# Both feed-forward layers as one level of Strassen, with streamed weights

## The chip, the cores and the metric

The kernel runs on one core of a Trainium2 chip. The metric is the device time of one execution in microseconds; the time shown for a kernel is the median of several executions. Engines are called as in the profile: PE (TensorE; PEld are its weight loads), DVE (VectorE), ACT (ScalarE), POOL (GpSimd) and SP (the queue from which nearly all DMAs are issued).

## What is computed

One step of a decoder layer: a prompt of 2048 tokens and eight single sample tokens go through an input projection, windowed attention, an mLSTM, an output projection and a feed-forward part, with norms between. The change touches the feed-forward part alone. Cut to that, with D_MODEL = 1024 and D_FF = 4096:

```python
x = x + jnp.concatenate([out_a, out_b], axis=-1) @ w_out
h2 = rmsnorm(x, norm2_g)
x = x + jnp.square(jax.nn.relu(h2 @ w_ff1)) @ w_ff2
...
y_prompt = rmsnorm(xp, final_g)
```

All of it is float32. The kernel splits each operand of a matmul into a high part (fp32r, made by ACT) and a low part (the remainder, made by DVE) and adds three matmuls: high by high, high by low and low by high.

## The kernel before

The order of each engine's instructions comes from a scheduler that starts from the order of the program text and from the buffers of the tile pools; each engine then runs its list in that order and waits on semaphores. `bufs=2` means that a name has two buffers in turn: the third tile of that name waits until the first one's readers are done.

The feed-forward part is `phase_c` (L1329). It first runs the output projection of the 16 token tiles of 128 (and one of 8), tile by tile, with the second norm and the transposes of tiles 0 to 7 woven in (`prep_norm`, `prep_move`). The transposed activations h2 stay in SBUF as high and low parts, for one half of the tokens at a time: tiles 0 to 7 as two blocks of 512 tokens, tiles 8 to 16 as blocks of 512, 256 and 264. Tiles 8 to 16 are prepared near the end of the first half's feed-forward work, in small jobs taken from a list (`bg`, `step`).

For each half there are 16 groups g of 256 hidden features. `ff1` (L1410) loads two tiles of w_ff1 (1024x128, 512 KB each, `load_ff`), splits them, and for each token block adds 8 x 3 matmuls in PSUM, applies relu on ACT (L1420), squares on DVE (L1421) and splits the result. `ff2` (L1429) loads two rows of w_ff2, and for each block and each of 8 output tiles adds 2 x 3 matmuls in PSUM; ACT copies the first group's sum to `acc` (L1440), and DVE adds the others' (L1442). ff1 of group g+1 stands ahead of ff2 of group g. A helper records all matmuls (L162 to L164) and splits (L158 on ACT, L159 on DVE).

After a half's last group, `finish` transposes `acc` back, adds the residual (L1457), takes the last norm on DVE (L1463) or on ACT and POOL (L1466), and stores the tile. The first half's tiles are finished inside the second half's work, the last tiles behind the last matmuls. POOL has nothing else to do in this part; in the parts before it, it does element-wise work on tiles of 128 to 640 columns.

## Time and profile before

| | us |
|---|---|
| median of 3 runs | 2720.64 |
| lowest and highest | 2719.99, 2722.58 |
| the profiled execution | 2713.16 |
| its span, first to last instruction | 2711.3 |
| PE busy | 2643.3 |
| DVE busy | 1459.7 |
| ACT busy | 840.4 |
| POOL busy | 200.2 |

The page gives busy times over the whole span, slices of a fortieth of the span each, and the chain that ended last. The view by stretches gives for each stretch its length, the busy time and number of instructions of each engine, the granted PE clock (1.00 is full), the share of time in which DMA engines moved data, and GB/s. In the views by group a row ends with the busy time, the mean duration in ns, and the idle time ahead of the group with what ended it. In the timeline a row begins with start and duration in us; "x2" means two instructions in a row taken together.

### The profile page before, as it was taken

The page shows a single profiled execution, that of the slowest core. Times are in us where ns is not written, and L with a number is a line of the kernel's source. Part 1 is how long each engine was busy: PE and PEld are TensorE (multiplying, and loading weights), DVE is VectorE, ACT ScalarE, POOL GpSimd, SP SyncE. Part 2 cuts the span into 40 slices and gives each one's busy share as a digit, 9 for nine tenths or more (in the row PEclk, how much of TensorE's full clock was granted, in tenths as well). Part 3 has the DMA queues.
Part 4 walks back from the last instruction along what each step waited for, and adds up shares of the span by engine and source line. Part 5 has one row for each costly group of instructions (what it writes and reads, how often), then busy time and mean ns, then how long its engine had stood idle before and what let it go on. Part 6 is the DMA issues. An engine that isn't in the chain of part 4 may idle for free.

```text
span 2711.3 us, 39662 instructions
## 1 busy us (share of the span) xinstructions
PE 2643.3 (97%) x15262; PEld 2333.0 (86%) x15262; DVE 1459.7 (54%) x3434; ACT 840.4 (31%) x1888; POOL 200.2 (7%) x198
## 2 busy tenths in 40 slices
PE   8999999999999989999999999999999999999997
PEld 7999999999788767887888888888889999999996
DVE  6324655665377566753345444444754545454547
ACT  5331224443345443322321212122452121212123
POOL 1000000000253242210000000000000000000001
PEclk9999999999799889999999999999999999999999
DMA  8575576656576565543222222111341111111113
GB/s 199 151 204 157 172 182 140 153 141 156 131 199 162 149 186 170 166 150 111 90 81 64 100 69 63 45 49 47 102 140 55 40 55 40 55 40 55 40 35 123
DMA packets 334225, 302.55 MB, mean 112 GB/s; under 512 B 108543, under 2 KB 301467, under 8 KB 331092
## 3 DMA queue, kind: packets, MB, share of 16 engines
q1 hardware_dynamic: 332212, 296.39, 38.5%
q0 software_dynamic: 1536, 3.10, 0.5%
q8 instruction: 120, 1.97, 0.3%
q14 instruction: 69, 0.57, 0.1%
q10 hardware_dynamic: 288, 0.53, 0.1%
HBM read 220.94 MB, written 95.17 MB: 117 GB/s over the span
## 4 chain that ended last, share of the span: by engine, by line
PE 89%; DVE 5%; DMA 3%; ACT 2%; issue 1%; POOL 0%; SPq 0%; DVEq 0%; ACTq 0%; POOLq 0%
PE pf L163 19%; PE pf L162 19%; PE pf L164 19%; PE pmm L162 5%; PE pmm L164 5%; PE pmm L163 5%; PE ps_s L1074 5%; PE po L1102 3%; PE pt L1087 2%; PE ptp L176 1%; PE ppq L367 1%; PE ppq L370 1%; DMA xt<-x_d 1%; DMA out_dram<-kt 0%; PE nu L459 0%
## 5 line engine op out<-in xcount | busy, mean ns | idle before, releaser
L1442 DVE TENSOR_TENSOR acc<-acc,pf 128x512 f32<-128x512 f32 (+2 forms) x600 | 343.4, 581 | 201.2 <-PE pf L164 200.0
L164 PE MATMUL pf<-rh,w2l 128*128 128x512 f32 (+2 forms) x1280 | 445.3, 348 | 0.0
L163 PE MATMUL pf<-rlo,w2h 128*128 128x512 f32 (+2 forms) x1280 | 445.0, 348 | 0.1
L162 PE MATMUL pf<-rh,w2h 128*128 128x512 f32 (+2 forms) x1280 | 444.4, 348 | 0.0
L162 PEld LDWEIGHTS pf<-rh,w2h 128*128 128x128 f32 x1280 | 241.8, 189 | 30.2 <-ACT rh L158 0.2
L163 PEld LDWEIGHTS pf<-rlo,w2h 128*128 128x128 f32 x1280 | 241.4, 189 | 30.6 <-DVE rlo L159 0.3
L164 PEld LDWEIGHTS pf<-rh,w2l 128*128 128x128 f32 x1280 | 241.3, 189 | 30.1 <-DVE w2l L159 0.2
L162 PE MATMUL pmm<-x,wh 128*128 128x344 f32 (+1 forms) x768 | 251.0, 327 | 0.0
L163 PE MATMUL pmm<-x,wh 128*128 128x344 f32 (+1 forms) x768 | 249.0, 324 | 0.0
L164 PE MATMUL pmm<-x,wl 128*128 128x344 f32 (+1 forms) x768 | 248.3, 323 | 0.0
L162 PE MATMUL pf<-h21h,w1h 128*128 128x512 f32 (+2 forms) x768 | 245.8, 320 | 0.0
L164 PE MATMUL pf<-h21h,w1l 128*128 128x512 f32 (+2 forms) x768 | 245.6, 320 | 0.0
L163 PE MATMUL pf<-h21l,w1h 128*128 128x512 f32 (+2 forms) x768 | 245.2, 319 | 0.0
L158 ACT ACTIVATE rh<-rl 128x264 fp32r<-128x264 f32 (+1 forms) x160 | 87.3, 546 | 465.8 <-PE pf L164 241.7
L163 PE MATMUL pf<-h20l,w1h 128*128 128x512 f32 x512 | 200.0, 391 | 0.0
L162 PE MATMUL pf<-h20h,w1h 128*128 128x512 f32 x512 | 200.0, 391 | 0.0
L164 PE MATMUL pf<-h20h,w1l 128*128 128x512 f32 x512 | 199.4, 390 | 0.0
L159 DVE TENSOR_TENSOR w1l<-w1r,w1h 128x1024 fp32r<-128x1024 f32 x64 | 78.4, 1226 | 186.0 <-ACT w1h L158 186.0
L1076 DVE CUSTOM_DVE_ANT_0 sm<-ps_s,nb 128x256 f32<-128x256 f32 (+1 forms) x288 | 100.0, 362 | 138.2 <-PE ps_s L1074 110.2
L1078 ACT ACTIVATE ex<-sm,R 128x256 f32<-128x256 f32 (+1 forms) x288 | 126.1, 459 | 144.1 <-DVE R L1076 140.3
L1421 DVE TENSOR_TENSOR rl<-rl 128x264 f32<-128x264 f32 (+1 forms) x160 | 93.3, 583 | 141.3 <-ACT rl L1420 141.3
L163 PEld LDWEIGHTS pf<-h21l,w1h 128*128 128x128 f32 x768 | 144.6, 188 | 12.8
(461 smaller groups left out, 5058.6 us busy)
## 6 DMA issues: line engine op xcount, KB each, us to landing
w1r<-in_w_ff_dram SPq DMA_DIRECT2D x64, 512.0 KB
w2r<-in_w_ff_dram SPq DMA_DIRECT2D x64, 512.0 KB
xt<-in_x_prompt_dram SPq DMA_DIRECT2D x31, 512.0 KB
xt<-x_d SPq DMA_DIRECT2D x25, 512.0 KB
R_d<-R SPq DMA_DIRECT2D x72, 132.0 KB
Rb<-R_d SPq DMA_DIRECT2D x48, 198.0 KB
V<-v_d SPq DMA_DIRECT2D x72, 130.0 KB
wraw<-in_w_in_dram SPq DMA_DIRECT2D x17, 512.0 KB
```

Source lines behind the costliest of these rows:

```text
L158: last_hi[0] = act.activation(hi, src, AF.Copy)
L159: last_lo[0] = (eng or vec).tensor_tensor(lo, src, hi.bitcast(F32), op=OP.subtract)
L162: pe.matmul(out, lh, rh, start=first, stop=False)
L163: pe.matmul(out, lh, rl, start=False, stop=False)
L164: pe.matmul(out, ll, rh, start=False, stop=last)
L1074: pe.matmul(out, Q[:, a:a + (P - 1) * d + 1:d], mv, start=i == 0, stop=i == 1)
L1076: vec.tensor_tensor_reduce(sm[:, :w], s_[:, e, c0:c0 + w], nb[:, o + bw - w:o + bw], 1.0, 3e38, OP.add, OP.min, mn)
L1078: act.activation(ex[:, e, :w], sm[:, :w], AF.Exp, bias=mn, scale=-1.0)
L1087: pe.transpose(pt[:, e, kb], ex[:, e, kb * P:(kb + 1) * P], ident)
L1102: pe.matmul(po[:, i + e], pT[:, e, kb], vts[kb], start=kb == 0, stop=kb == nk - 1)
L1421: vec.tensor_tensor(r[:, :n], r[:, :n], r[:, :n], op=OP.mult)
L1442: vec.tensor_tensor(av, av, pf[:, :n], op=OP.add)
```

## The change

Both layers become, for each half of the tokens (now 1024 and 1032), one level of Strassen's scheme. A matrix product of 2x2 blocks is made from 7 products of sums and differences of blocks, in place of 8. The features are worked off in two chunks of 2048, so that a chunk's first layer is a product of 2048 x 1024 (weights) by 1024 x tokens, and its second of 1024 x 2048 by 2048 x tokens, each cut in halves on all sides. What follows from that:

- Weights are streamed: each "step" of 24 matmuls (48 in the second half, whose blocks of 516 tokens are cut in two of 258) loads one or two blocks of 128x1024 (`a_load`, names `ax` and `ay`, two buffers each), adds or subtracts them on POOL where the product asks for two (`combine`; 5 of 7 products), and splits the sum into `ah` and `al`, three buffers each. A product has four steps.
- Activations: h2 of all tiles is made in the output projection and stored to DRAM (`h2_d`). In the first layer each product loads two pieces of 256 rows x half the tokens of one or two blocks (`b_load`, `bx` two buffers, `by` one), adds them on POOL where there are two, and splits them (`b_prep`, `bh` and `bl`, four buffers each). In the second layer the pieces are sums of the hidden blocks `R`, four per product, without loads.
- `ahead(s)` stands before step s: it prepares weights up to step s+2, loads up to s+3, and prepares up to two activation pieces when the piece four before it is used up.
- Results: each product's sum in PSUM is added to or subtracted from one or two blocks of the result (12 in all for 7 products), the first time by a copy on ACT, later on DVE (`put`). Blocks of the first layer get relu and square when complete, two of the four on ACT, two in one instruction on DVE (L1515 of the new kernel, both inputs in SBUF).
- The orders of the products are 5, 1, 2, 3, 6, 4, 7 in the first layer and 5, 3, 1, 2, 6, 4, 7 in the second.

```diff
-    CBLK = (((0, 512), (512, 512)), ((1024, 512), (1536, 256), (1792, 264)))
+    PROD_A = {1: ((0, 0), (1, 1), 1), 2: ((1, 0), (1, 1), 1), 3: ((0, 0), None, 0), 4: ((1, 1), None, 0),
+              5: ((0, 0), (0, 1), 1), 6: ((1, 0), (0, 0), -1), 7: ((0, 1), (1, 1), -1)}
+    PROD_B = {1: ((0, 0), (1, 1), 1), 2: ((0, 0), None, 0), 3: ((0, 1), (1, 1), -1), 4: ((1, 0), (0, 0), -1),
+              5: ((1, 1), None, 0), 6: ((0, 0), (0, 1), 1), 7: ((1, 0), (1, 1), 1)}
...
+    ORDER = {1: (5, 1, 2, 3, 6, 4, 7), 2: (5, 3, 1, 2, 6, 4, 7)}
+    SB = ((0, 512, 1), (1024, 516, 2))
...
+        def a_load(s):
...
+            for (r, q), name in zip([x for x in blocks[:2] if x], ("ax", "ay")):
+                x = wst.tile([P, 4 * 256], F32, name=name, bufs=2)
...
+        def combine(tl, sign):
+            if len(tl) > 1:
+                gp.tensor_tensor(tl[0], tl[0], tl[1], op=OP.add if sign > 0 else OP.subtract)
+            return tl[0]
...
+        def a_split(s):
+            d = steps[s]
+            x = combine(d.pop("raw"), PROD_A[d["p"]][2])
+            h = wst.tile([P, 4 * 256], F32R, name="ah", bufs=3)
+            l = wst.tile([P, 4 * 256], F32R, name="al", bufs=3)
+            split(h, l, x)
...
+        def b_prep(j):
...
+            if u_["ph"] == 1:
+                x = combine(u_.pop("raw"), blocks[2])
+            else:
+                tl = [R[b, u_["j"]][:, :, :W] for b in blocks[:2] if b]
+                x = tl[0]
+                if len(tl) > 1:
+                    x = wst.tile([P, 2, 516], F32, name="bx", bufs=2)[:, :, :W]
+                    gp.tensor_tensor(x, tl[0], tl[1], op=OP.add if blocks[2] > 0 else OP.subtract)
+            h = wst.tile([P, 2, 516], F32R, name="bh", bufs=4)
+            l = wst.tile([P, 2, 516], F32R, name="bl", bufs=4)
+            split(h[:, :, :W], l[:, :, :W], x)
...
+        def ahead(s):
+            while nxt["raw"] < min(s + 4, len(steps)) and nxt["raw"] < nxt["split"] + 2:
+                a_load(nxt["raw"])
+                nxt["raw"] += 1
+            while nxt["split"] < min(s + 3, nxt["raw"]):
+                a_split(nxt["split"])
...
+            for _ in range(2 if s else 4):
+                j = nxt["bprep"]
+                if j == len(bunits) or bunits[j]["first"] > s + 4 or (j >= 4 and bunits[j - 4]["last"] >= s):
+                    break
...
+        def put(dst, src, sign, new, nb):
...
+            if new:
+                act.activation(dst, src, AF.Copy, scale=float(sign))
+            else:
+                vec.tensor_tensor(dst, dst, src, op=OP.add if sign > 0 else OP.subtract)
...
+                        if (blk, p) in (((0, 1), 3), ((1, 0), 4)):
+                            act.activation(cv, cv, AF.Relu)
+                            act.activation(cv, cv, AF.Square)
+                        elif (blk, p) in (((1, 1), 6), ((0, 0), 7)):
+                            vec.scalar_tensor_tensor(cv, cv, 0.0, cv, op0=OP.max, op1=OP.mult)
```

The order shows what this makes of two engines. On POOL, before, the last element-wise work of the output projection (`Rb`) is followed directly by the last norm of the final tiles (`xt`), with the whole feed-forward part between them:

```order
L346 TENSOR_TENSOR Rb_13218<-Rb_13218,dw 128x6x65
L346 TENSOR_TENSOR Rb_13220<-Rb_13220,dw 128x6x65
L346 TENSOR_TENSOR Rb_13325<-Rb_13325,dw 128x6x65
L346 TENSOR_TENSOR Rb_13327<-Rb_13327,dw 128x6x65
L346 TENSOR_TENSOR Rb_13432<-Rb_13432,dw 128x6x65
L346 TENSOR_TENSOR Rb_13434<-Rb_13434,dw 128x6x65
L1466 TENSOR_TENSOR xt_24987<-xt_24987,fg 128x1024
L1466 TENSOR_TENSOR xt_24989<-xt_24989,fg 128x1024
```

On POOL, after, in the second layer of the first half's first chunk, weight sums (`ax`) alternate with activation sums made from the hidden blocks (`bx` from two `R`; the numbers tell the tiles apart):

```order
L1444 TENSOR_TENSOR bx<-R_14068,R_14244 128x2x512
L1444 TENSOR_TENSOR bx<-R_14109,R_14284 128x2x512
L1409 TENSOR_TENSOR ax<-ax,ay 128x1024 x2
L1444 TENSOR_TENSOR bx<-R_13988,R_14164 128x2x512
L1444 TENSOR_TENSOR bx<-R_14029,R_14204 128x2x512
L1444 TENSOR_TENSOR bx<-R_14070,R_14244 128x2x512
L1444 TENSOR_TENSOR bx<-R_14111,R_14284 128x2x512
L1444 TENSOR_TENSOR bx<-R_13988,R_13986 128x2x512
L1409 TENSOR_TENSOR ax<-ax,ay 128x1024 x3
```

There are 280 such sums over the feed-forward part, where there were none.

On DVE, before, in the second half, low parts of weights (`w1l`, `w2l`) and of hidden blocks (`rlo`), squarings (`rl`) and result additions (`acc`) follow each other like this:

```order
L159 TENSOR_TENSOR w2l<-w2r,w2h 128x1024
L1421 TENSOR_TENSOR rl<-rl 128x512
L159 TENSOR_TENSOR rlo_19702<-rl,rh_19701 128x512
L1421 TENSOR_TENSOR rl<-rl 128x256
L159 TENSOR_TENSOR rlo_19734<-rl,rh_19733 128x256
L159 TENSOR_TENSOR w1l<-w1r,w1h 128x1024
L1421 TENSOR_TENSOR rl<-rl 128x264
L159 TENSOR_TENSOR rlo_19766<-rl,rh_19765 128x264
L1421 TENSOR_TENSOR rl<-rl 128x512
L1421 TENSOR_TENSOR rl<-rl 128x256
L159 TENSOR_TENSOR w1l<-w1r,w1h 128x1024
L1442 TENSOR_TENSOR acc<-acc,pf_19883 128x512
```

On DVE, after, in the second layer of the first half, low parts of weight sums (`al`) and of activation sums (`bl`) stand in runs between the result additions:

```order
L160 TENSOR_TENSOR bl<-bx,bh 128x2x512
L160 TENSOR_TENSOR al<-ax,ah 128x1024
L1479 TENSOR_TENSOR acc<-acc,pf_15853 128x512
L1479 TENSOR_TENSOR acc<-acc,pf_15860 128x512
L1479 TENSOR_TENSOR acc<-acc,pf_15867 128x512
L1479 TENSOR_TENSOR acc<-acc,pf_15874 128x512
L160 TENSOR_TENSOR al<-ax,ah 128x1024
L160 TENSOR_TENSOR bl<-bx,bh 128x2x512 x4
L160 TENSOR_TENSOR al<-ax,ah 128x1024
L1479 TENSOR_TENSOR acc<-acc,pf_16007 128x512
```

Each `al` or `bl` with a sum ahead of it waits for that sum on POOL and for the high part on ACT, and the additions behind it on DVE wait with it.

More of the change, by code (lines that the diff above doesn't have):

```diff
@@ new lines, in ahead @@
+        def ahead(s):
[4 more added lines that the diff above has]
+                a_split(nxt["split"])
+                nxt["split"] += 1
+                if nxt["raw"] < min(s + 4, len(steps)):
+                    a_load(nxt["raw"])
+                    nxt["raw"] += 1
+            for _ in range(2 if s else 4):
+                j = nxt["bprep"]
+                if j == len(bunits) or bunits[j]["first"] > s + 4 or (j >= 4 and bunits[j - 4]["last"] >= s):
+                    break
+                if nxt["bload"] == j:
+                    b_load(j)
+                    nxt["bload"] += 1
+                b_prep(j)
+                nxt["bprep"] += 1
+                if j + 1 < len(bunits) and bunits[j + 1]["first"] <= s + 6:
+                    b_load(j + 1)
+                    nxt["bload"] += 1
@@ new lines, in half, with final @@
+        def half(xt, acc, base, t, i):
+            t0, n = t * P, P if t < NT else NB
+            pt = pst.tile([P, 4, P], F32, name="ptp", tag="t")
+            for k in range(4):
+                pe.transpose(pt[:n, k], acc[:, 4 * i + k, t0 - base:t0 - base + n], ident)
+            xv = xt[:n, 512 * i:512 * i + 512]
+            vec.tensor_tensor(xv, xv, pt[:n].rearrange("p k d -> p (k d)"), op=OP.add)
+        def final(xt, t, alt=False):
+            t0, n = t * P, P if t < NT else NB
+            jk = stg.tile([P, D], BF16, name="jkc", bufs=1)
+            ss = small.tile([P, 1], F32, name="ss")
+            act.activation(jk[:n], xt[:n], AF.Square, accum_out=ss[:n])
+            r = rms_rstd(ss[:n], n, D)
+            if alt:
+                act.activation(xt[:n], xt[:n], AF.Copy, scale=r[:n])
+                gp.tensor_tensor(xt[:n], xt[:n], fg[:n], op=OP.mult)
+            else:
+                vec.scalar_tensor_tensor(xt[:n], xt[:n], r[:n], fg[:n], op0=OP.mult, op1=OP.mult)
+            nc.sync.dma_start(O["y_prompt"][0, t0:t0 + n] if t < NT else O["y_sample"][:, 0], xt[:n])
@@ L1508, in phase_c @@
-        blocks = nblocks
-        sres.close()
-        pres = pool(st, "res", 3, "left")
-        res = ff1(blocks, 0, pres)
-        for g in range(NG):
-            if g + 1 < NG:
-                nxt = ff1(blocks, g + 1, pres)
-            if g == 0:
-                while bg:
-                    step()
-                acc = ml.tile([P, KD, 1032], F32, name="acc", bufs=1)
-            if g + 1 == NG:
-                sh2.close()
-                fin = pool(st, "fin", 9, "right")
-                xts = [fetch(fin, t) for t in range(8, NT + 1)]
-            ff2(blocks, g, res, acc, 1024,
-                (lambda t: finish(xts[t - 8], acc, 1024, t)) if g + 1 == NG else None)
-            res = nxt
+        rp = pool(st, "rp", 1, "left")
@@ L1526, in phase_c @@
+        for _ in copies:
+            pass
         st.close()
```

317 lines of the change are left out of this document (187 added, 130 removed).

## Prediction

> **What bounds the kernel now.** I read the page's busy times, slices and chain first.
>
> ```profile
> PE 2643.3 (97%) x15262; PEld 2333.0 (86%) x15262; DVE 1459.7 (54%) x3434; ACT 840.4 (31%) x1888; POOL 200.2 (7%) x198
> ...
> POOL 1000000000253242210000000000000000000001
> PEclk9999999999799889999999999999999999999999
> ...
> PE 89%; DVE 5%; DMA 3%; ACT 2%; issue 1%; POOL 0%; SPq 0%; DVEq 0%; ACTq 0%; POOLq 0%
> ```
>
> TensorE (PE) carries 89% of the chain that ended last, at full granted clock from the 16th slice on; GpSimd (POOL) does nothing there until the end. The view by stretches shows the feed-forward stage: first half, second half, end, tail, with two inner stretches from which a matmul is priced.
>
> ```profile
> core 0: us, PE busy (x) PEld busy (x) DVE busy (x) ACT busy (x) POOL busy (x), PEclk, DMA share, GB/s
> 1117.00:1200.00 83.00, 83.00 (x386) 68.20 (x385) 53.87 (x156) 24.14 (x67) 13.89 (x15) 1.00 0.54 170
> 1247.00:1960.00 713.00, 713.00 (x3154) 585.84 (x3152) 345.42 (x491) 171.03 (x258) 0.00 (x0) 1.00 0.23 74
> 1300.00:1400.00 100.00, 100.00 (x440) 82.22 (x439) 44.28 (x58) 26.85 (x39) 0.00 (x0) 1.00 0.27 88
> 1960.00:2640.00 680.00, 677.15 (x4368) 619.93 (x4367) 339.13 (x619) 166.75 (x305) 0.00 (x0) 1.00 0.18 57
> 2100.00:2400.00 300.00, 300.00 (x1922) 274.57 (x1921) 150.44 (x271) 61.30 (x103) 0.00 (x0) 1.00 0.15 46
> 2640.00:2694.00 54.00, 53.75 (x357) 48.35 (x357) 39.39 (x86) 16.67 (x34) 7.13 (x3) 1.00 0.27 99
> 2694.00:2711.30 17.30, 3.23 (x20) 1.95 (x18) 13.00 (x26) 4.96 (x13) 4.85 (x2) 0.67 0.46 182
> ```
>
> From 1247 to 2694 PE waits for about 3 us in 1447. VectorE (DVE) is busy half of the time, ScalarE (ACT) a quarter, DMA a fifth. So this stage is PE's, and whatever takes matmuls out of it pays in full, as long as the others keep up.
>
> **The change: matmuls.** Before, the first half has 2 layers x 2 blocks x 32 x 8 x 3 = 3072 matmuls of 512 columns, the second 1536 each of 512, 256 and 264. The third stretch gives 100/440 = 0.2273 us per 512 columns; the fifth 300/1922 = 0.1561 on the mean of the three widths, 0.4683 per triple, so 0.2410 for 256+264. Sum: 3072 x 0.2273 + 1536 x 0.4683 = 698.3 + 719.3 = 1417.6 us. After, each half has 2 chunks x 2 layers x 7 products x 96 = 2688 matmuls: of 512 columns in the first half, 611.0 us, and as pairs of 258 in the second, 0.2410 x 516/520 = 0.2391 a pair, 642.7 us. PE is freed of 1417.6 - 1253.7 = 163.9 us.
>
> Moved at no net cost: the norms and transposes of tiles 8 to 16 go from the feed-forward stage into the output projection. PE does them in either place; DVE's 53.87 and ACT's 24.14 us of 83 leave room there. The first new matmuls stand directly behind the projection's in PE's order, and the last tile's transposes are put among them. The tail stays: five tiles of closing norm behind the last matmul, as now (17.3 us).
>
> **Operands.** Each block sum is one addition of 128x1024 on POOL before the split into a high part (ACT) and a low part (DVE). Their rows and those of the result additions:
>
> ```profile
> L1442 DVE TENSOR_TENSOR acc<-acc,pf 128x512 f32<-128x512 f32 x360 | 244.3, 686 | 149.4 <-PE pf L164 148.2
> L159 DVE TENSOR_TENSOR w1l<-w1r,w1h 128x1024 fp32r<-128x1024 f32 x64 | 78.4, 1226 | 186.0 <-ACT w1h L158 186.0
> L158 ACT ACTIVATE w1h<-w1r 128x1024 fp32r<-128x1024 f32 x64 | 67.9, 1061 | 153.7 <-PE pf L163 152.0 <-DMA w1r<-in_w_ff_dram 1.7
> L1421 DVE TENSOR_TENSOR rl<-rl 128x512 f32<-128x512 f32 x96 | 66.1, 688 | 111.9 <-ACT rl L1420 111.9
> ```
>
> Counted in the order: 280 additions on POOL, 392 low splits and 64 squarings on DVE, 416 result additions on DVE (which read PSUM and SBUF). What POOL costs, and what it does to DVE, shows only at the end of before; POOL's rows, then DVE's:
>
> ```profile
> 2678.49 4.76 POOL L1466 TENSOR_TENSOR xt<-xt,fg 128x1024 f32<-128x1024 f32 x2 [1480.10 <-ACT xt L1465]
> ...
> 2694.06 2.50 POOL L1466 TENSOR_TENSOR xt<-xt,fg 128x1024 f32<-128x1024 f32 x1 [7.16 <-ACT xt L1465]
> 2698.69 2.35 POOL L1466 TENSOR_TENSOR xt<-xt,fg 128x1024 f32<-128x1024 f32 x1 [2.13 <-ACT xt L1465]
> ```
>
> ```profile
> 2679.02 0.69 DVE L1442 TENSOR_TENSOR acc<-acc,pf 128x512 f32<-128x512 f32 x1 [0.67 <-PE pf L164]
> ...
> 2681.12 2.15 DVE L154 TENSOR_TENSOR rs_o<-rs_y,rs_a 8x1 f32<-8x1 f32 x1
> ...
> 2694.35 2.23 DVE L148 SCALAR_TENSOR_TENSOR rs_a<-rs_y,rs_v 128x1 f32<-128x1 f32 x1
> ...
> 2697.35 0.21 DVE L148 SCALAR_TENSOR_TENSOR rs_a<-rs_y,rs_v 128x1 f32<-128x1 f32 x1
> ...
> 2699.14 2.99 DVE L1463 SCALAR_TENSOR_TENSOR xt<-xt,rs_o,fg 128x1024 f32<-128x1024 f32 x1
> ...
> 2703.94 1.29 DVE L1463 SCALAR_TENSOR_TENSOR xt<-xt,rs_o,fg 128x1024 f32<-128x1024 f32 x1
> ```
>
> One POOL operation is 4.76/2 = 2.38 us. A DVE operation with both inputs in SBUF that comes during one runs only once it has ended: L148 is 2.23 instead of 0.21 us and ends with POOL's (2696.58 against 2696.56), L1463 is 2.99 instead of 1.29. The addition that reads PSUM is not held (0.69 in the middle of POOL's 4.76). So POOL's sums, DVE's low splits and squarings take turns, and only the 416 result additions run beside POOL. Altogether 280 x 2.38 + 392 x 1.226 + 64 x 0.688 = 666 + 481 + 44 = 1191 us of turns for 1254 us of matmuls: 95%, a very tight fit.
>
> By product (PE: 96 x 0.2273 = 21.82 us in the first half, 22.95 in the second). Layer 1 has 4 weight and 2 activation splits, 7.36 us; POOL sums are 6 (products 1, 6, 7), 4 (5, 2) or 2 (3, 4); products 6 and 7 add 8 squarings, 5.50. Turns: 27.1 us for 6 and 7, 21.6 for 1, 16.9 or less for the rest. Layer 2 has 8 splits, 9.81 us, and 8 POOL sums in products 1, 6, 7: 28.85 us; 4 in the others: 19.33. A product takes the larger of PE and turns if operands prepared ahead bridge nothing, and this is the value I take, since the loops prepare weights at most three steps ahead and a product has four; smoothing over a layer is the other end. Excess: layer 1, 2 products x 2 chunks x (5.32 + 4.19) = 38.0; layer 2, 3 x 2 x (7.03 + 5.90) = 77.6; together 115.6 us. If a whole layer is smoothed, turns are 133.9 and 163.9 us against 152.7 and 160.7 of PE: only layer 2 exceeds, 2 x 11.2 + 2 x 3.2 = 29 us.
>
> One more wait: in layer 2 of the second half, product p+1's activation halves take over buffers that product p releases one step (5.74 us) before they are needed. ACT 1.06 + 3 low splits 3.68 = 4.74 us, with one POOL operation in the way 7.12. I take half of the 1.4 us over, 14 times: 10 us (bounds 0 and 14 x 4 = 56, with two POOL operations in the way).
>
> Transfers: in layer 1 a step needs 12/7 x 0.524 = 0.90 MB of weights and 0.45 MB of activations in 5.46 us, 247 GB/s.
>
> ```profile
> 1721.78 0.38 SPq L1395 DMA_DIRECT2D w1r<-in_w_ff_dram  x1
> ```
>
> ```profile
> DMA  0000000000000032236799999510000000000000
> GB/s 0 0 0 0 0 0 0 0 0 0 0 0 0 0 92 84 59 79 207 220 323 348 340 330 356 154 56 0 0 10 8 10 10 15 0 0 0 0 0 0
> ```
>
> One 0.52 MB load, issued at 1721.78, runs at some 345 GB/s in rows of 512 bytes (slices of 0.2 us from 1720) and is in at about 1725.2, 3.4 us later; the new rows are 1 or 2 KB. Hidden, with a quarter to spare.
>
> **Sum.** Span 2711.3 - 163.9 + 115.6 + 10 = 2673.0 us. The profiled execution took 2713.16, 1.9 more than its span, and the median shown is 7.5 above that: 2682 us.
>
> **Rivals.**
> *Lookahead smooths it*: sums may lie in raw tiles (two for weights, two for activations) until their split is due, 4 x 2.38 = 9.5 us of turns in hand against 4 to 7 us of excess per product. Then the span is 2711.3 - 163.9 + 29 = 2576, a median of 2586; with PE never waiting, 2557. For it: split tiles have buffers of their own. Against: three queues that each run in order must hand over without a gap at 95%.
>
> *The weight buffers' round trip* (slower): a two-block step's raw tile has two buffers. Round: load 3.4 + 1.5 for the second block, a POOL operation ahead 2.38, its own 2.38, ACT 1.06, one POOL operation in DVE's way 2.38, DVE 1.23 = 14.3 us, 7.17 per step against 5.6 of PE. Over the 160 two-block steps 251 us: span 2798, median 2808. It decides against the change from 164/160 = 1.02 us per step on, a round of 13.2 us; without any waiting the round is 9.6. For it: the next load cannot start before the low split is done. Against: both waits at full length in each round is much.
>
> *The clock*:
>
> ```profile
> 0.00:400.00 400.00, 382.81 (x2441) 373.06 (x2442) 199.69 (x499) 135.49 (x304) 14.03 (x29) 1.00 0.65 176
> 400.00:800.00 400.00, 393.52 (x2522) 361.70 (x2521) 241.39 (x886) 168.90 (x438) 51.49 (x51) 0.95 0.64 153
> ```
>
> Clock was lost (0.95) in a stretch where PE idled for 6.5 us, and not in one where it idled for 17, so how the waits are cut decides, not their sum. At 0.95 throughout, 1253.7 us of matmuls take 66 more: median 2748, slower. For it: PE's new waits of up to 7 us per product. Against: they can fall apart into several small ones, and the first stretch lost nothing with more. The Trainium skill (TensorE: Matmul & The Clock Gate, Part 1) has the clock at half after an idle window of about 3.4 us. By that an excess taken in one piece costs clock and one taken in small waits nothing, with which the two rows agree.
>
> *It doesn't do what it says*: the order has 8064 matmuls for 7680, with 12.5% fewer columns, so it does, unless pairs of 258 with the same weights expose their weight loads. At the fifth stretch's 274.57/1921 = 0.143 us each, 5376 would take 768 us instead of 643: median 2807. Against: that stretch has as many loads, all hidden.
>
> **Chances.** Forecast 0.55, of which 0.05 lies so far up that it can't be told from no change; smoothing 0.18; round trip 0.20; clock 0.05; exposed loads 0.02. Faster 0.50 + 0.18 = 0.68, same 0.05, slower 0.27. The bound for "same" is 0.2%, 5.4 us, about what a measurement of this kernel tells from no change. The forecast's own range is 2624 to 2728: from half of its 115.6 us smoothed away, to the activation wait at 56 instead of 10. Over all 2585 to 2795: it takes in the smoothed case and most of the round trip's ways short of its full length; left out are PE without waits and a round as long as priced or longer.
>
> **What would show it.** Right: PE busy for 1254 us and the transposes in a feed-forward stage of about 1400; POOL busy by some 670 us there; low splits well over 1.226 us on the mean while additions from PSUM stay near 0.69; layer 2 losing more than layer 1. Wrong: PE waiting first on loads of the raw weights (the round trip), low splits at 1.23 us on the mean (no turns), clock under 1.00, or equal loss in both layers.

## The result and the profile after

The changed kernel takes 2892.76 us (median of 4, 2892.12 to 2894.28) against 2721.61 us before: a ratio of 1.063, 95% interval 1.0611 to 1.0648. The forecast was 2682 us in a range of 2585 to 2795. It was wrong in its direction and outside its range.

Lines of the page of the changed kernel; the numbers to hold against those of before are PE's share and the granted clock from the 18th slice on, where the feed-forward stage begins.

```profile
PE 2601.1 (90%) x15646; PEld 2318.5 (80%) x15646; DVE 1747.7 (60%) x3227; ACT 1083.5 (37%) x2077; POOL 934.9 (32%) x475
...
PE   8999999999999898999877889899898978898986
...
POOL 1000000001542423203335444356443455433552
PEclk9999999998999889999989899999899989999998
```

The feed-forward stage alone, from the first new matmul to the last one, in the view by stretches (PE, PEld, DVE, ACT, POOL busy, PE's clock, DMA share, GB/s):

```profile
1283.20:2869.40 1586.20, 1380.47 (x8189) 1223.41 (x8187) 994.39 (x959) 573.89 (x727) 726.46 (x273) 0.93 0.52 169
2869.40:2890.70 21.30, 3.28 (x23) 2.15 (x21) 12.31 (x29) 8.74 (x22) 5.25 (x2) 0.67 0.31 123
```

PE is idle for 1586.2 - 1380.5 = 205.7 us there, which it had been for 3 us before. And its 1380.5 busy us are longer than the matmuls need: a run without waits (e1 below) has the same matmuls in 1283.4. So 97.1 us more went in a lower clock. No engine is full: DVE is busy for 63% of the stage, ScalarE (ACT) 36%, POOL 46%, DMA 52%. They wait for each other. The view of waits in the stage: who waited, for whom, us in all, times, longest. PE first, then POOL, then the sync queue (SPq), which issues all loads in order.

```profile
PE pf L1528 <- ACT ah L159: 32.6, 7, 8.3
PE pf L1528 <- DVE bl L160: 26.3, 17, 3.7
PE pf L1494 <- DVE R L1479: 21.9, 14, 5.9
PE pf L1494 <- DVE al L160: 21.5, 15, 4.3
...
POOL ax L1409 <- DMA ax<-in_w_ff_dram: 292.2, 55, 61.8
POOL bx L1444 <- DVE bl L160: 178.5, 51, 12.3
POOL bx L1409 <- DMA by<-h_d: 67.6, 18, 10.9
...
SPq L1403 <- POOL ax L1409: 430.2, 67, 17.9
SPq L1397 <- POOL ax L1409: 218.2, 45, 9.4
SPq L1403 <- DVE al L160: 210.1, 64, 17.2
SPq L1397 <- DVE al L160: 204.9, 68, 14.4
```

It is a ring. The sync queue cannot load because POOL has not taken the sum out of the raw tile, or DVE not its low part; POOL cannot add because the load is not there. PE's waits are spread over high parts, low parts and result tiles, because whichever link is late when PE arrives is named. One turn of this ring, around PE's wait of 8.2 us at 1585.68, in the timeline (start, duration, instruction, idle time before it and what ended it); POOL, then the sync queue, ACT, DVE and PE:

```profile
1574.39 2.40 POOL L1444 TENSOR_TENSOR bx<-R,R 128x1024 f32<-128x1024 f32 x1 [7.39 <-DVE bl L160]
1579.90 2.34 POOL L1444 TENSOR_TENSOR bx<-R,R 128x1024 f32<-128x1024 f32 x1 [3.12 <-DVE bl L160]
1582.20 4.66 POOL L1409 TENSOR_TENSOR ax<-ax,ay 128x1024 f32<-128x1024 f32 x2
1591.60 2.39 POOL L1409 TENSOR_TENSOR ax<-ax,ay 128x1024 f32<-128x1024 f32 x1 [4.74 <-DMA ax<-in_w_ff_dram]
...
1569.79 15.14 SPq L1403 DMA_DIRECT2D ay<-in_w_ff_dram  x2
1587.96 0.37 SPq L1403 DMA_DIRECT2D ax<-in_w_ff_dram  x1
...
1577.51 1.06 ACT L159 ACTIVATE bh<-bx 128x1024 fp32r<-128x1024 f32 x1 [4.46 <-PE pf L1528]
1584.57 1.06 ACT L159 ACTIVATE ah<-ax 128x1024 fp32r<-128x1024 f32 x1 [6.00 <-POOL ax L1409]
...
1578.59 1.23 DVE L160 TENSOR_TENSOR bl<-bx,bh 128x1024 fp32r<-128x1024 f32 x1 [4.29 <-ACT bh L159]
...
1585.68 0.79 PE L1528 MATMUL pf<-bh,ah 128*128 128x512 f32 x1 [8.21 <-ACT ah L159]
```

Two activation sums (`bx`) stand ahead of the weight sum (`ax`) in POOL's list and wait for a buffer that DVE's low split releases. That split in turn waits for ACT's high part, which starts at 1577.51, when PE's own last matmuls have released its buffer. So the wait is a chain from PE back to PE without a load in it: high part 1.06, low split 1.23, activation sum 2.34, the first of the two weight sums about 2.3 (from 1582.20 on), high part 1.06 (from 1584.57 on), together 8.0 of the 8.2 us; PE follows at 1585.68. The stage's other two waits of 8.2 us (to 1497.49 and 1620.60) are the same chain, and the DMA engines are busy for at most 1% of each. Of all 73 waits over 1 us (192.4 us), 20 with 64.7 us pass with the DMA engines under 5% busy; in the others loads are under way. Meanwhile the second of the two loads that the queue issues from 1569.79 on has stood there for some 15 us, with every load behind it; so the next sum waits for a load (4.74 us), and the ring goes round again.

What the wait costs after it has ended is in PE's next rows:

```profile
1588.58 0.63 PE L1528 MATMUL pf<-bh,ah 128*128 128x512 f32 x1
1589.01 0.63 PE L1528 MATMUL pf<-bl,ah 128*128 128x512 f32 x1
1589.43 0.63 PE L1528 MATMUL pf<-bh,al 128*128 128x512 f32 x1
...
1593.20 0.40 PE L1528 MATMUL pf<-bh,al 128*128 128x512 f32 x1
1593.44 0.39 PE L1528 MATMUL pf<-bh,ah 128*128 128x512 f32 x1
1593.67 0.40 PE L1528 MATMUL pf<-bl,ah 128*128 128x512 f32 x1
```

Matmuls start 0.42 to 0.43 us apart until 1592.85, and 0.23 apart from 1593.20 on: half the clock for some 7 us after the wait, with a second wait of 1.09 us among them. The Trainium skill (TensorE: Matmul & The Clock Gate, Part 1) gives 426.7 ns between matmuls of 512 columns for an array throttled to half its clock by an idle window; the trace agrees, at 0.43.

### The profile page after: what moved, and what is told of

It is laid out like the page before. It is cut to its first block, busy times and chain, and to the rows that moved or that the text cites. A ratio compares the mean times of both kernels' runs of the same rounds, so it can differ in the third digit from the quotient of the medians.

```text
span 2890.7 us, 41837 instructions
## 1 busy us (share of the span) xinstructions
PE 2601.1 (90%) x15646; PEld 2318.5 (80%) x15646; DVE 1747.7 (60%) x3227; ACT 1083.5 (37%) x2077; POOL 934.9 (32%) x475
## 5 line engine op out<-in xcount | busy, mean ns | idle before, releaser
L1409 POOL TENSOR_TENSOR ax<-ax,ay 128x1024 f32<-128x1024 f32 x160 | 415.0, 2596 | 582.9 <-DMA ax<-in_w_ff_dram 292.2
L160 DVE TENSOR_TENSOR al<-ax,ah 128x1024 fp32r<-128x1024 f32 x224 | 367.8, 1643 | 344.1 <-ACT ah L159 343.4
L159 ACT ACTIVATE ah<-ax 128x1024 fp32r<-128x1024 f32 x224 | 236.6, 1058 | 629.8 <-POOL ax L1409 477.0
L1528 PE MATMUL pf<-bh,ah 128*128 128x258 f32 (+1 forms) x1344 | 376.1, 335 | 70.6 <-ACT ah L159 32.6
L1494 PE MATMUL pf<-bh,ah 128*128 128x258 f32 (+1 forms) x1344 | 372.9, 332 | 53.5 <-DVE R L1479 21.9
L1528 PE MATMUL pf<-bl,ah 128*128 128x258 f32 (+1 forms) x1344 | 375.1, 334 | 26.3 <-DVE bl L160 26.3
L1494 PE MATMUL pf<-bh,al 128*128 128x258 f32 (+1 forms) x1344 | 370.3, 330 | 21.5 <-DVE al L160 21.5
L1528 PE MATMUL pf<-bh,al 128*128 128x258 f32 (+1 forms) x1344 | 371.7, 332 | 7.7 <-DVE al L160 7.7
L1494 PE MATMUL pf<-bl,ah 128*128 128x258 f32 (+1 forms) x1344 | 367.9, 328 | 0.4 <-DVE bl L160 0.4
L1528 PEld LDWEIGHTS pf<-bh,ah 128*128 128x128 f32 x1344 | 236.1, 200 | 97.9 <-ACT ah L159 35.8
L160 DVE TENSOR_TENSOR bl<-bx,bh 128x1024 fp32r<-128x1024 f32 (+1 forms) x136 | 235.3, 1732 | 112.4 <-ACT bh L159 112.0
L1494 PEld LDWEIGHTS pf<-bh,ah 128*128 128x128 f32 x1344 | 232.4, 197 | 81.7 <-ACT ah L159 23.1
L1528 PEld LDWEIGHTS pf<-bl,ah 128*128 128x128 f32 x1344 | 236.3, 200 | 50.6 <-DVE bl L160 30.5
L1494 PEld LDWEIGHTS pf<-bh,al 128*128 128x128 f32 x1344 | 231.3, 196 | 49.7 <-DVE al L160 30.0
L1528 PEld LDWEIGHTS pf<-bh,al 128*128 128x128 f32 x1344 | 235.6, 199 | 32.4 <-DVE al L160 12.1
L1494 PEld LDWEIGHTS pf<-bl,ah 128*128 128x128 f32 x1344 | 232.6, 196 | 21.7 <-DVE bl L160 0.9
```

Of the source, the lines that this page charges most:

```text
L159: last_hi[0] = act.activation(hi, src, AF.Copy)
L160: last_lo[0] = (eng or vec).tensor_tensor(lo, src, hi.bitcast(F32), op=OP.subtract)
L1409: gp.tensor_tensor(tl[0], tl[0], tl[1], op=OP.add if sign > 0 else OP.subtract)
L1494: pe.matmul(pf[:, n, :w], x_, y_[:, n * w:n * w + w], start=fst, stop=lst)
L1528: pe.matmul(pf[:, n, :w], x_[:, i, dsl], y_[:, n * w:n * w + w], start=a, stop=b)
```

## The experiments

**Theory A** is the forecast's: POOL and DVE take turns at the port, and PE waits for the turns. **Theory B** is the second rival's: the round trip of a raw weight buffer (load, sum, split, release) is longer than the matmuls that it feeds. All runs are compared with the kernel before on the same chip, and each row's stage is that of its own profiled execution. Idle is PE's idle time in the stage, clock is PE's busy time beyond e1's 1283.4 us.

| run | what | median us | ratio to before (95%) | stage us | idle | clock |
|---|---|---|---|---|---|---|
| changed kernel | | 2892.8 | 1.063 (1.0611 to 1.0648) | 1586.2 | 205.7 | 97.1 |
| e1 | no preparation | 2582.0 | 0.9485 (0.9469 to 0.9502) | 1283.4 | 0.0 | 0.0 |
| e2 | no weight loads | 2650.2 | 0.9737 (0.9721 to 0.9753) | 1348.8 | 43.7 | 21.8 |
| e3 | sums on DVE | 2682.9 | 0.9856 (0.9836 to 0.9877) | 1394.5 | 68.9 | 42.2 |
| e4 | no sums but layer 2's activations | 2637.2 | 0.9684 (0.9658 to 0.971) | 1347.1 | 39.5 | 24.2 |
| e5 | sums earlier in the text | 2886.2 | 1.0592 (1.057 to 1.0614) | 1592.9 | 206.2 | 103.3 |
| e6 | e5 and a third raw buffer | 2855.5 | 1.049 (1.0468 to 1.0511) | 1551.1 | 174.9 | 92.8 |
| e7 | e2 and e3 | 2574.4 | 0.9455 (0.9434 to 0.9477) | 1283.6 | 0.0 | 0.2 |
| e8 | e3 and e6 | 2704.0 | 0.9937 (0.9918 to 0.9956) | 1413.4 | 83.5 | 46.5 |
| e9 | one load a step | 2722.4 | 1.0002 (0.9986 to 1.0018) | 1420.6 | 93.3 | 44.0 |
| e10 | no cache copies | 2825.7 | 1.0376 (1.0348 to 1.0404) | 1530.1 | 162.2 | 84.5 |
| e11 | e3, no cache copies | 2584.6 | 0.9499 (0.9476 to 0.9522) | 1294.0 | 8.1 | 2.5 |
| **e12** | **e3, copies in quarters** | **2587.0** | **0.9508 (0.9485 to 0.9531)** | 1296.8 | 7.4 | 6.0 |
| m1 | copies in quarters | 2748.8 | 1.0106 (1.0078 to 1.0133) | 1455.1 | 115.8 | 55.9 |
| m2 | m1, weight sums on DVE | 2654.1 | 0.9756 (0.9729 to 0.9783) | 1359.7 | 52.0 | 24.3 |
| m3 | m1, activation sums on DVE | 2658.7 | 0.9782 (0.9745 to 0.9818) | 1366.5 | 56.5 | 26.6 |
| m4 | e12, moved norms left out | 2572.2 | 0.9456 (0.9432 to 0.948) | 1295.9 | 8.1 | 4.4 |
| n1 | order of the text held | 3013.9 | 1.1083 (1.1061 to 1.1104) | 1715.0 | 324.0 | 107.7 |
| n2 | n1, copies in quarters | 3012.3 | 1.1081 (1.1052 to 1.1109) | 1715.9 | 325.0 | 107.5 |

One thing must be known to read it. The scheduler orders each engine's instructions anew for every kernel, so an edit that takes a transfer away also moves other instructions. By their POOL lists (480 rows) the runs with sums on POOL differ from the changed kernel by 34 rows (e10), 40 (e9), 52 (e6 and m1), 70 (e2) and 76 (n1), and n1 shows below that the order alone can be worth 129 us. So what these runs show is the edit together with the order that came with it.

### The floor, and each suspect alone (e1 to e4)

e1, three split weight tiles for all steps, four activation tiles per half:

```
         def ahead(s):
...
+            steps[s]["w"] = fl[s % 3]
...
-                bu = [bunits[d["b0"] + j]["x"] for j in range(2)]
+                bu = [fl["b", (d["b0"] + j) % 4] for j in range(2)]
...
-                        bh, bl = bunits[d["b0"] + f // 2]["x"]
+                        bh, bl = fl["b", (d["b0"] + f // 2) % 4]
```

> Leaves out the preparation of operands in the feed-forward stage: three split weight tiles and, in each half, four split activation tiles are reused for all steps; matmuls, result additions, squarings, norms and output stay. It measures what the stage costs when TensorE never waits for an operand. If the matmuls are priced rightly (1253.7 us) and the clock is lost only behind waits: a stage of about 1275 us at clock 1.00 and a span near 2575 to 2590 us. If the clock falls for another reason, or pairs of 258 columns expose their weight loads: 2650 us or more.

```profile
1274.60:2558.00 1283.40, 1283.40 (x8196) 1165.94 (x8195) 370.02 (x579) 198.37 (x348) 4.84 (x2) 1.00 0.07 24
```

PE is never idle, at full clock. The forecast's stage without waits is 1446.5 - 163.9 = 1282.6 us; measured 1283.4. The stage without waits stands, pairs of 258 columns cost what was said, and the clock falls only with waits. That the two agree within 1 us is partly luck: by the starts of their records, the matmuls take 1270.4 us here and 1427.7 before, so that 157.3 us are freed and not 163.9, and some 6 us of other work (transposes that were moved ahead, idle time) left the stage as well.

e2, the raw tiles of the first two steps are used throughout:

```
+                if (name, s % 2) in kept:
+                    tl.append(kept[name, s % 2])
+                    continue
-                x = wst.tile([P, 4 * 256], F32, name=name, bufs=2)
+                x = kept[name, s % 2] = wst.tile([P, 4 * 256], F32, name=name, bufs=2)
```

> Leaves out the loads of weights after the first two steps: the raw tiles stay where they are and are added, split and used again in the same order with the same number of operations; activations are still loaded. Theory A (taking turns at the port between GpSimd and VectorE is what TensorE waits for): the operations on both engines are the same, so the time stays within 30 us of the changed kernel's 2893 us. Theory B (the round trip of the two raw buffers, the load being one leg of it): about 5 us of each 14 us round go, and most of the roughly 200 us of waits with them: below 2740 us.

The groups of POOL's weight sums and of DVE's low splits (busy us, mean ns, idle before and what ended it):

```profile
L1412 POOL TENSOR_TENSOR ax<-ax,ay 128x1024 f32<-128x1024 f32 x160 | 451.5, 2823 | 382.2 <-DVE al L160 359.8
L160 DVE TENSOR_TENSOR al<-ax,ah 128x1024 fp32r<-128x1024 f32 x224 | 403.5, 1801 | 86.2 <-ACT ah L159 85.7
L160 DVE TENSOR_TENSOR bl<-bx,bh 128x1024 fp32r<-128x1024 f32 (+1 forms) x136 | 277.8, 2044 | 78.2 <-ACT bh L159 77.7
```

Theory A would have kept the time; 2650 us is B's number. The turns are all there, and longer than in the changed kernel (a weight sum 2.82 against 2.60 us, a weight's low split 1.80 against 1.64), yet stage and floor differ by 65.4 us only. So turns at the port are worth at most that where no weight loads are in the ring.

e3, sums on DVE:

```
-                gp.tensor_tensor(tl[0], tl[0], tl[1], op=OP.add if sign > 0 else OP.subtract)
+                vec.tensor_tensor(tl[0], tl[0], tl[1], op=OP.add if sign > 0 else OP.subtract)
...
-                    gp.tensor_tensor(x, tl[0], tl[1], op=OP.add if blocks[2] > 0 else OP.subtract)
+                    vec.tensor_tensor(x, tl[0], tl[1], op=OP.add if blocks[2] > 0 else OP.subtract)
```

> All 280 block sums move from GpSimd to VectorE (1.23 us there by the row of the low splits, instead of 2.6 to 2.8), loads unchanged. VectorE then has 392 splits + 280 sums at 1.23, 64 squarings and 416 result additions at 0.69: 1153 us for 1254 us of matmuls, with nobody to take turns with. Theory A: most of the waits go: 2650 to 2750 us. Theory B: the round trip gets shorter too (8 to 10 us instead of 14), 2700 to 2800. A time at or above 2893 us would mean that neither the port nor the length of the sum matters.

2683 us: in theory A's range; B's began at 2700. It computes everything, and is faster than the kernel before. The loads have their part in what is left: with sums on DVE and no loads (e7) nothing is left.

e4:

```
         def combine(tl, sign):
-            if len(tl) > 1:
-                gp.tensor_tensor(tl[0], tl[0], tl[1], op=OP.add if sign > 0 else OP.subtract)
             return tl[0]
```

> Leaves out the 160 weight sums and the 40 activation sums of layer 1 (the first block alone is used); both blocks are still loaded; the 80 activation sums of layer 2 stay on GpSimd. Theory A: turns fall from 1191 us to about 720 us, waits nearly gone: 2600 to 2660 us. Theory B: the round loses the sum (2.4 us) and its wait, and is 9 to 10 us against 11.2 us of matmuls for two steps: 2600 to 2700 us. If what is late is the transfers themselves, time stays above 2800.

2637 us, again within both: with all loads and 80 sums left on POOL, 63.7 of the 302.8 us remain.

### Buffers and order (e5 to e8)

e5, the sum of step s + 3 ahead of `b_prep` in the text:

```
-            x = combine(d.pop("raw"), PROD_A[d["p"]][2])
+            x = d.pop("sum")
...
+            sums(min(s + 4, nxt["raw"]))
             for _ in range(2 if s else 4):
```

> Order alone: each step's weight sum is issued on GpSimd a step earlier, ahead of the activation sums that now stand before it; same work, same buffers. If weight sums are late because they stand in GpSimd's queue behind activation sums that wait for their buffer: 2780 to 2850 us instead of 2893. If the load's length in a round with two raw buffers is what counts, wherever the sum stands: 2870 to 2910.

The edit did nothing: the lists of instructions of all five engines are row for row those of the changed kernel, since the scheduler sorts by its own rules. 2886 us is the changed kernel once more and tests neither theory.

e6, e5's edit and this one, with the pool of `hs` moved to make room:

```
-                x = wst.tile([P, 4 * 256], F32, name=name, bufs=2)
+                x = (deep[0].tile([P, 4 * 256], F32, name="ax3") if deep and name == "ax" and s % 3 == 2
+                     else wst.tile([P, 4 * 256], F32, name=name, bufs=2))
...
-            while nxt["raw"] < min(s + 4, len(steps)) and nxt["raw"] < nxt["split"] + 2:
+            while nxt["raw"] < min(s + 4 + len(deep), len(steps)) and nxt["raw"] < nxt["split"] + 2 + len(deep):
```

> As the run before, and a third raw buffer for the first block, so that its load is issued a step (5.5 us) earlier. Theory B (round trip of the raw buffers): the round may now take three steps, 16.8 us, for the first block; the waits for weights mostly go: 2690 to 2780 us. Theory A (turns at the port): nothing is taken from the turns, so no gain beyond the run before.

2856 us, a gain of 30 where B expected over 100. A third raw buffer for the first block (`ax`) is not what was missing. The second block's was not tried: in the changed kernel the sync queue waits longest, 648 us, for POOL to release an `ay` buffer, and still 673 us here. So B as a matter of depth is not settled.

e7, the edits of e2 and e3 together:

> No weight loads after the first two steps, and all sums on VectorE: against the run without loads (2650 us) it gives the price of taking turns at the port alone. Of the 65 us that stage lost over the floor (1348.8 against 1283.4): theory A at its smaller size says nearly all: 2590 to 2605 us. If VectorE, now with 1153 us of work in order, is as late as the turns were: 2640 us or more.

```profile
1269.00:2552.60 1283.60, 1283.59 (x8196) 1166.02 (x8195) 1100.80 (x1233) 575.66 (x729) 0.00 (x0) 1.00 0.18 57
```

2574 us, below theory A's range even: the floor, with DVE busy for 86% of the stage. Without POOL the low splits are back at 1.223 us. 1348.8 - 1283.6 = 65 us is what the sums cost on POOL where no weights are loaded: the port, POOL's longer sum and another order together.

e8, the edits of e3, e5 and e6 together:

> All three together, nothing left out: sums on VectorE, weight sums issued a step earlier, third raw buffer for the first block. If the two causes are separate, the price of the round trip that is left in the run with sums on VectorE (2683 us, some 80 us over the same without loads) falls by half or more: 2610 to 2650 us, under both kernels. If VectorE's queue in order is what holds the loads, little changes: 2670 to 2690.

2704 us, worse than e3's 2683 and outside both expectations. A third buffer for the first block does not help here either.

### The loads and the cache copies (e9 to e12)

e9:

```
-            for (r, q), name in zip([x for x in blocks[:2] if x], ("ax", "ay")):
+            for (r, q), name in zip([x for x in blocks[:1] if x], ("ax", "ay")):
...
-            d["raw"] = tl
+            d["raw"] = tl * (2 if blocks[1] else 1)
```

> The changed kernel with one load per step instead of up to two: the second block is not loaded, the first is added to itself on GpSimd; sums, splits and their order are unchanged, 160 of 384 weight loads are left out. If the load of the second block, which stands behind the first one's in the sync queue and waits for GpSimd to release its buffer, is the leg that makes the round long: 2680 to 2760 us, near the 2650 us without loads. If one load in the round costs as much as two (its latency, not its bytes): 2820 us or more.

2722 us, in the first theory's range: with 160 of 384 loads out of the queue, and 40 rows of POOL's list changed, 165.6 of the 302.8 us go.

e10:

```
             for b in range(NB):
-                tc.keep_in_program_order(nc.sync.dma_start(ov[b, 0:511], sv[b, 1:512]))
-                yield
+                pass
```

> The changed kernel without the 16 copies of 766 KB of the cached keys and values (left out, their outputs are not written), which are issued on the same queue, one a product, through the first 16 products of the first half. If they are what makes loads late, the first half's stage loses 60 us or more of its waits and the time falls to 2800 to 2830. If the round without them is as long: 2870 to 2893, no change in the second half in either case.

2826 us, 67 less than the changed kernel, in the first expectation's range, and in the first half alone: it takes 724.4 instead of 784.3 us, the second 805.7 instead of 801.9. But POOL's list is another one too, so this doesn't show that the copies' transfers made the difference. e11 is e10 with sums on DVE:

> Sums on VectorE, and the 16 copies left out. In the run with sums on VectorE TensorE waits and loses clock from 1300 to 1800 us, where the copies are issued, and hardly after. If the copies do that: 2590 to 2620 us instead of 2683. If it is the first half's wider loads, or activation loads in the same queue: above 2650.

In e3 the loss lies where the copies are issued, as its stretches and the copies' first and last issue show:

```profile
1300.00:1800.00 500.00, 441.03 (x1746) 345.34 (x1745) 343.32 (x369) 191.62 (x235) 0.00 (x0) 0.92 0.57 190
1800.00:2600.00 800.00, 790.07 (x5778) 752.96 (x5777) 689.65 (x774) 349.16 (x430) 0.00 (x0) 1.00 0.64 201
...
L623 SPq DMA_DIRECT2D out_dram<-in_cache_win_k_dram x8: 520/526/634, 1130.3 to 1486.6; - x8
L623 SPq DMA_DIRECT2D out_dram<-in_cache_win_v_dram x8: 515/516/521, 1514.1 to 1708.6; - x8
```

In this stretch (to 1730 us) 55.7 of PE's 57.8 us of waits are for a weight's high part on ACT. One of them in full: a row of stretches ahead of the wait and one of the wait, then ACT's, DVE's and PE's rows:

```profile
1552.20:1558.50 6.30, 6.29 (x28) 4.80 (x26) 2.45 (x2) 1.06 (x1) 0.00 (x0) 1.00 0.00 0
1558.50:1564.40 5.90, 0.00 (x0) 0.00 (x0) 3.59 (x3) 2.12 (x2) 0.00 (x0) 0.94 0.01 4
...
1558.53 1.06 ACT L159 ACTIVATE bh<-bx 128x1024 fp32r<-128x1024 f32 x1 [4.46 <-PE pf L1528]
1563.32 1.06 ACT L159 ACTIVATE ah<-ax 128x1024 fp32r<-128x1024 f32 x1 [3.73 <-DVE ax L1409]
...
1559.62 1.23 DVE L160 TENSOR_TENSOR bl<-bx,bh 128x1024 fp32r<-128x1024 f32 x1 [3.03 <-ACT bh L159]
1560.88 1.22 DVE L1444 TENSOR_TENSOR bx<-R,R 128x1024 f32<-128x1024 f32 x1
1562.02 1.22 DVE L1409 TENSOR_TENSOR ax<-ax,ay 128x1024 f32<-128x1024 f32 x1
...
1564.43 0.80 PE L1528 MATMUL pf<-bh,ah 128*128 128x512 f32 x1 [5.94 <-ACT ah L159]
```

It is the changed kernel's chain once more, from PE's last matmuls to PE, with DVE doing the sums. The transfers stand still (DMA share 0.00, then 0.01) and have for at least 6 us when PE begins to wait: the weights are there, and their sum stands in DVE's list behind work that waits for PE. So it is in 13 of e3's 18 waits over 1 us, 51.6 of 63.9 us: the DMA engines are under 5% busy. And in e11's list, which the copies' absence alone makes different, 33 of the first half's 80 weight sums stand ahead of result additions that they stand behind in e3, and none the other way; in the second half there is no such difference.

Without the copies e11 is at 2585 us, just below its first expectation and 10.6 us of stage above the floor. e12 does the whole work:

```
-                tc.keep_in_program_order(nc.sync.dma_start(ov[b, 0:511], sv[b, 1:512]))
-                yield
+                for a in range(0, 512, 128):
+                    e = min(a + 128, 511)
+                    tc.keep_in_program_order(nc.sync.dma_start(ov[b, a:e], sv[b, a + 1:e + 1]))
+                    yield
...
-            if d["end"] and sb == 0:
+            if s % 3 == 2:
                 next(copies, None)
```

> Nothing left out: sums on VectorE, and each cache copy issued as four of 192 KB, one every third step over both halves instead of one of 766 KB a product in the first half. If a copy hurts by standing for 2 us or more on every transfer engine ahead of a load, a quarter of it at a time fits in the rounds' slack: 2600 to 2640 us, under both kernels. If only the bytes count: near 2683.

```profile
1268.80:2565.60 1296.80, 1289.38 (x8188) 1168.02 (x8187) 1097.26 (x1232) 579.16 (x727) 0.00 (x0) 1.00 0.63 207
```

2587 us, below both expectations and 4.9% under the kernel before: two edits turn the loss into a gain of 134 us, most of what the matmuls promise. All weights are loaded, at 207 GB/s, and PE waits for 7.4 us.

### What is left with sums on POOL (m1 to n2)

m1 is the changed kernel with e12's copies:

> The changed kernel with sums on GpSimd as it was, and each cache copy cut in four, one quarter every third step over both halves; nothing left out. If the size of one copy is what hurts: like the run without copies, 2815 to 2840 us. If, with no slack in the round, the quarters hurt as much spread out: 2860 to 2890.

2749 us, far below what either theory had, and 77 us below e10, which has no copies at all. Fewer transfers cannot be slower by themselves; the order differs (POOL's list of 480 rows has 52 lines of difference to the changed kernel's, 36 to e10's). Over the floor, the four kernels that do the whole work lose 302.8 us (changed kernel), 171.7 (m1), 111.1 (e3) and 13.4 (e12): sums on POOL make 158 to 192 us of it, whole copies with the order that goes with them 98 to 131.

m2, and m3 with the same argument in the two activation sums instead:

```
-        def combine(tl, sign):
+        def combine(tl, sign, eng=gp):
...
-            x = combine(d.pop("raw"), PROD_A[d["p"]][2])
+            x = combine(d.pop("raw"), PROD_A[d["p"]][2], vec)
```

> Copies in quarters; the 160 weight sums on VectorE, the 120 activation sums stay on GpSimd; nothing left out. Round trip: no sum on GpSimd stands in the weights' round any more, only 120 operations that hold the port: 2600 to 2660 us. Turns in total: 120/280 of the loss that GpSimd's sums make between 2587 and the run before: near 2690 us.

> Copies in quarters; the 160 weight sums on GpSimd, the 120 activation sums on VectorE; nothing left out. Round trip: the weights' round is as long as in the changed kernel, less activation sums ahead of it in GpSimd's queue: 2740 to 2830 us. Turns in total: 160/280 of that loss: near 2720 us, only 30 us above the run with the other 120 sums there.

2654 and 2659 us: m2 is in the round trip's range, m3 below both of its expectations. The weights' sums on POOL cost no more than the activations', which speaks against B in the form "the sum inside the weights' round is what counts". Over the floor, m2 loses 76.3 us, m3 83.1, both kinds together (m1) 171.7, neither (e12) 13.4. Above e12 that is 62.9 + 69.7 = 132.6 apart and 158.3 together: roughly additive, with some 26 us more where both are in one list.

m4, e12 with:

```
-            prep_norm(xt, n)
-            moving = (xt, t, n)
+            if t < 8:
+                prep_norm(xt, n)
+                moving = (xt, t, n)
```

> The complete kernel with sums on VectorE and copies in quarters (2587 us), with the norms and transposes of tiles 8 to 16, which the change moved into the output projection, left out (the second half works on activations of the first). If moving them there is what delays the stage's start from 1247 to some 1270 us: start at 1245 to 1252 us, total 2560 to 2570. If the start comes from the first operands' preparation at tile 13: no earlier than 1262, total 2575 or more.

The stage starts at 1254.8 instead of 1268.8 us and the time is 2572 us: between the two expectations. From 1000 us to the stage's start PE is busy for 10.8 us less and idle for 3.2 us less than in e12, so most of the 14 us is PE's own time for work that m4 leaves out. The changed kernel and e5, with one order, start at 1283.2 and 1272.0, so this number is good to some 10 us only.

n1 holds the order of the text on POOL, the loads, DVE and ACT in the stage (the last two through `pinned`, lines 62 to 78); n2 adds e12's copies:

```
-                gp.tensor_tensor(tl[0], tl[0], tl[1], op=OP.add if sign > 0 else OP.subtract)
+                tc.keep_in_program_order(gp.tensor_tensor(tl[0], tl[0], tl[1], op=OP.add if sign > 0 else OP.subtract))
...
         acc = None
+        pinned[0] = True
```

The two have the same lists on DVE, ACT, POOL and the sync queue, copies aside.

> The changed kernel, same work, buffers, engines and copies, with the order of the text held in the feed-forward stage: on GpSimd each step's weight sum stands before the activation sums of the units due four steps later, where the scheduler had put runs of up to eight weight sums behind up to four activation sums. If the order on GpSimd and of the loads is a cause of its own: 2760 to 2830 us instead of 2893. If the round with GpSimd's sum in it is too long in any order: 2870 us or more.

> As the run before, on VectorE, ScalarE, GpSimd and for the loads in exactly its order, with each cache copy cut in four, a quarter every third step. If the copies' size delays loads whatever the order: 40 to 80 us below the run before (with sums on VectorE the copies' effect was near 96 us, but mixed with the order). If what the quarters did was to change the order: within 15 us of the run before.

```profile
1270.30:2985.30 1715.00, 1391.05 (x8189) 1236.64 (x8188) 1048.15 (x959) 577.41 (x727) 743.65 (x273) 0.90 0.48 159
```

```profile
1267.80:2983.70 1715.90, 1390.94 (x8188) 1236.05 (x8187) 1045.92 (x959) 577.49 (x727) 740.41 (x273) 0.90 0.48 159
```

n1 lies in the range of its second expectation (too long in any order), but not for its reason: the order of the text costs 129 us of stage more than the scheduler's, with the same work, buffers and engines. So the order in the lists is a cause of its own, of the size of the others here, and holding the text's order was no cure. n2 is n1's time, as expected if the quarters work by the order: in one order, cutting the copies changes nothing.

## Why the prediction was wrong, point by point

The forecast's span was 2673.0 us, the measured one 2890.7. The 217.7 us between are: the stage's start 35.7 (1283.2 against 1247.5), the floor 0.8, waits 80.1 (205.7 against 125.6 forecast), clock 97.1, the tail 4.0 (21.3 against 17.3). In the terms of the sum, the waits were priced too low and as the wrong kind of wait, the clock was put at nothing and is the largest item, and the moved norms were put at nothing as well.

- **Matmuls, -163.9 us: right.** e1 has the stage without waits within 1 us of it; the matmuls alone freed 157.3 us, and the rest of the agreement is luck (see e1). The rival of exposed weight loads is out.
- **"A product takes the larger of PE and turns", +115.6 us: this step failed.** The turns are there, and their signs came: low splits at 1.64 us on the mean, additions from PSUM at 0.68, POOL busy for 726 us, layer 2's lines waiting more than layer 1's. But e2 against e7 puts POOL's sums without weight loads, clock included, at 65 us, nearer to the forecast's smoothed 29 than to 115.6, and PE waited for 205.7 us. The rule adds up busy time by product. The waits that could be followed are chains in time instead: PE's last matmuls free a buffer, a split and a sum for later work run, and only then comes the sum that PE needs, with its weights already there (8.2 us at 1585.68, and 5.94 us in e3 without POOL and without turns). What stands ahead of a sum in its engine's list was no term of the forecast.
- **"The weight buffers' round trip" as a rival apart, 0.20, 2808 us: this step failed.** It was weighed as an alternative to the turns, and "both waits at full length in each round is much" spoke against it. In the trace it is one ring with them: loads wait for sums, sums for loads and for activation buffers, splits for the port. Taking out loads (e2), sums (e4) or POOL (e3) each removes 190 us or more of the 302.8, so the shares cannot be added as if separate. Nor is it the rival's own picture: a third raw buffer for the first block gave 30 us (e6), and weight sums on POOL cost no more than activation sums (m2, m3).
- **"Hidden, with a quarter to spare": this step failed too.** It held the mean rate of the transfers against their peak. The stage moves only 169 GB/s, and e12 moves 207 with PE fed. So the rate is not what makes loads late. What was missed is that one queue issues all loads in order and stops at the first buffer that is not free, for up to 17.9 us at a time.
- **The clock, a rival at 0.05, priced at 66 us: it is 97.1 us and not apart from the rest.** It came with the waits: in the runs with over 30 us of idle time, 0.33 to 0.61 us of clock for each us of it. By the changed kernel's own 0.47 a forecast with 126 us of waits should have carried 59 us of clock, which alone takes 2682 above the time of before. The prediction counted on small waits costing no clock, by the 3.4 us of an idle window; the trace says otherwise. PE is busy without a gap to 1529.4 and then waits once, for 2.15 us, and the clock is at half for the 3.4 us behind it:

```profile
1524.00:1529.40 5.40, 5.40 (x24) 4.10 (x22) 1.22 (x1) 1.05 (x1) 2.42 (x1) 1.00 0.00 0
1531.58:1535.00 3.42, 3.42 (x8) 2.77 (x9) 1.39 (x2) 0.00 (x0) 3.08 (x1) 0.51 0.23 75
...
1531.58 0.77 PE L1528 MATMUL pf<-bh,ah 128*128 128x512 f32 x1 [2.15 <-ACT ah L159]
```

- **"Moved at no net cost": this failed too.** From 1000 us to the stage's start PE is busy for 20.1 us more than before (work that left the stage among them) and idle for 23.7 us instead of 8.1; this is the later start of 35.7 us. The projection's transposes (L1361) wait for DVE's norms, 15.1 us in the rows below. m4 gives 14 us for the work of tiles 8 to 16 itself, of which the stage gets some 6 back. How much of the rest is the move and how much differs from build to build was not separated.

```profile
PE ptp L1361 <- DVE xt L171: 6.7, 4, 3.2
PE ptp L1361 <- DVE mn L336: 5.0, 4, 1.5
PE ptp L1361 <- DVE rs_a L149: 3.4, 1, 3.4
```

**What stays open.** With sums on DVE the copies make the last 100 us (e3 against e11 and e12). The trace of e3 says that it is mostly the order that they lead the scheduler to and not their bytes, and n1 and n2 agree; a run with sums on DVE in one fixed order, with and without copies, would show it and was not made. For the changed kernel it is not settled how the 302.8 us divide among the order on POOL, POOL's longer sums, the port and late loads: waits with the transfers standing still make a third of its longer waits, and for m1's 77 us below e10 no other candidate than the order was found.

## What to carry to other kernels

Before pricing a stage by each engine's busy time, draw the ring that a buffer goes through (load, sum, split, release) and ask what stands ahead of each link in its engine's list, above all work that itself waits for the matmuls: here no helper was over two thirds busy and PE still lost 303 us. Price the clock with the waits: in these runs each microsecond of PE waiting brought 0.33 to 0.61 us of it. And a slow helper engine is no relief when its work stands in that ring: DVE does the sum in 1.22 us and POOL in 2.4 to 3.1, so giving 280 sums to the busier engine made the kernel faster by 210 us.

## What was not expected of the hardware

- DVE carries 1097 us of work in 1297 us (e12), in order, with PE waiting for 7.4 us: 85% on the helper was no bottleneck where POOL did nothing. By the Trainium skill (SBUF — State Buffer, Who interferes with whom) POOL and DVE hold the shared port in turn; the low split's 1.22 us without POOL and 1.64 to 2.04 with it agree. With all 280 sums on POOL and no weight loads the stage lost 65 us.
- A wait of 2.15 us was enough to halve the clock for 3.4 us (to 1535.00). After 8.2 us of waiting PE ran at half its clock for some 7 us, so one late tile cost it some 3 us more behind the wait (14 matmuls at 0.43 instead of 0.23).
- Two profiled executions of the changed kernel's instruction lists (its own and e5's) have stages of 1586.2 and 1592.9 us and starts that differ by 11.2 us; differences of that size between builds mean little.
